# A hybrid decoder layer on one core: two loads on another queue, norms and gates behind minima, output products between turned tiles

## The chip, the cores and the metric

The kernel runs on one core of one Trainium2 chip. The metric is the device time of one execution in microseconds (us), the median over runs. The engines are named as in the profile: PE is TensorE, DVE is VectorE, ACT is ScalarE, POOL is GpSimd, SP is SyncE, which here only issues transfers.

## What is computed

One decoder layer for 1024 tokens of width 1024, all in float32:

```
xn  = rmsnorm(x);  proj = xn @ w_in          # one combined input projection
A:  8 heads, sliding window of 128, ALiBi, sinks, QK-norm, 2 kv heads
B:  8 heads, causal, logits + c[t] - c[s], c = cumsum(log_sigmoid(gate)), QK-norm
h   = x + concat[A, B] @ w_out
y   = h + relu(rmsnorm(h) @ w_up)^2 @ w_down
```

## The kernel before, in words

**Precision.** TensorE multiplies rounded operands. Each operand is therefore split: `hi` is the rounded value, `lo` the rest (`split`, line 75: a cast on one engine, line 77 or 79, and a subtraction on another, line 80). A product is three matmuls: hi x hi, hi x lo and lo x hi, each on a block of 128 x 128 weights.

**Stages, in order of time.**
- To about 38 us: x is loaded, scaled and split; the first part of the input projection (`w_a0`) fills eight PSUM banks `qps`, one for each block of 128 tokens. They are then copied to `q0` (line 227), on VectorE and ScalarE in turn.
- To about 79 us: `load_w` (line 237) brings the second weight `w_a1` in eight pieces. A piece is a load into a raw buffer `wr` (three buffers, issued by SP, line 241), a cast on ScalarE and a low part on GpSimd. `wa1_tile` (line 455) then makes the products of one block of tokens, 24 matmuls `ps`, copies the result to `q3`, and after every second block calls `qknorm` (line 266): a square on GpSimd (line 279), a sum on VectorE (line 284), a reciprocal root on ScalarE and VectorE, a multiplication on GpSimd (line 310). `make_q_a` and `make_k_a` turn (transpose on TensorE, then split) the normed heads. Meanwhile x is loaded again, row by row (`xq`, line 413), and squared for its norm.
- To about 318 us and on to 427 us: attention, in units. A unit is a score part (`scores_a`, `scores_b`: matmuls into one of two `sc` banks, then on VectorE the minimum of score plus bias, lines 544 and 699, then an exponential on ScalarE) and a mix part (`mix_a`, `mix_b`). `mix_b` takes the probabilities 256 keys at a time: up to four turns into one of three `tr` banks (line 740), `evict_pt` (a cast on ScalarE, line 402, and a low part on VectorE, line 403), then products with V into `pvb`. The mix parts run two units behind the scores (`pend`, `drain`, `DEPTH`). The last four units have 2, 4, 1 and 3 such steps (`ORDER_END`), on one head.
- `fillers` is a list of other work with a count of units from which each piece may be traced: the projections of the B heads (`project_b`) and the first half of the output products (`out_first`, over mixed tiles 0 to 3).
- To about 465 us: the second half of the output products (`out_products`, 24 matmuls `po` for one output tile, over mixed tiles 4 to 7), with `out_weights` (line 869) for their weights: a load into one of two raw buffers, a cast on ScalarE, a low part on GpSimd. `out_finish` (line 991) adds and splits h.
- From 465 us: the two products of the MLP, in a scheme with seven sub-products.

**Mixed tiles.** The mixed values of tiles 0 to 6 go through memory: `split_mix` (line 602) loads a tile, multiplies it by the reciprocals (`make`, line 624, on VectorE), splits it (ScalarE, GpSimd; there is one buffer `mixs` for the low half) and stores it; `load_mix` brings it back when TensorE wants it. `heads_b` runs one step of each tile's list for each unit. The last tile, 7, is split in place (line 763, ScalarE and VectorE).

**What sets the order.** Each engine runs its queue in order. The order is worked out by a scheduler that simulates expected times: of what is ready, it takes what has the highest priority, which is the order of the program, moved forward by `tc.high_priority(offset=...)`. `tc.issue_after(ins)` puts the instructions in its block behind `ins` on the engine of `ins`; it adds no wait of its own. So every edit of the program can move the order elsewhere too.

**Around the change.** Lines 227 to 229 copy `q0` and free the first banks; line 407 loads `w_a1`; line 463 calls `qknorm` after each second block; `start_a` (line 510) sets out the first stage; `forget_gates` (line 466) starts with an addition on VectorE, line 467; lines 934 to 957, at the end of attention, hold the start of the second output half:

```
    fill(True)
    mix6 = load_mix(6)
    ...
    beside(0, marks[-1], 4, 5)     # 12 products behind the last scores
    beside(1, ended[-1], 4)        # 6 behind the products of the last unit but two
    drain(1)
    beside(1, ended[-1], 5)
    drain(0)
```

## Time and profile before

| what | value |
|---|---|
| median of three runs | 1084.01 us (1082.84 to 1084.91) |
| the profiled execution | 1082.51 us |
| its span in the trace | 1080.8 us |
| matmuls on PE, and its busy time | 5492, 1070.7 us (99%) |
| busy time of DVE, ACT, POOL | 780.2, 573.4, 383.2 us |
| bytes moved | 195.93 MB, mean 181 GB/s |

A row of a view gives a start, a duration, the engine, the line of the kernel, the operation, what it writes and reads, and in brackets the idle time of the engine before it and what ended it. Rows of matmuls overlap, since they are pipelined; their count over the time that they fill gives their pace. In the table by stages each engine has its busy time and, in brackets, its number of instructions, in the order PE, PEld (weight loads), DVE, ACT, POOL; behind them stand the granted clock, the share of the DMA engines and their GB/s.

### The profile page before, as it was taken

The page shows a single profiled execution, that of the slowest core. Times are in us where ns is not written, and L with a number is a line of the kernel's source. Part 1 is how long each engine was busy: PE and PEld are TensorE (multiplying, and loading weights), DVE is VectorE, ACT ScalarE, POOL GpSimd, SP SyncE. Part 2 cuts the span into 40 slices and gives each one's busy share as a digit, 9 for nine tenths or more (in the row PEclk, how much of TensorE's full clock was granted, in tenths as well). Part 3 has the DMA queues.
Part 4 walks back from the last instruction along what each step waited for, and adds up shares of the span by engine and source line. Part 5 has one row for each costly group of instructions (what it writes and reads, how often), then busy time and mean ns, then how long its engine had stood idle before and what let it go on. Part 6 is the DMA issues. An engine that isn't in the chain of part 4 may idle for free.

```text
span 1080.8 us, 15581 instructions
## 1 busy us (share of the span) xinstructions
PE 1070.7 (99%) x5492; PEld 930.5 (86%) x5492; DVE 780.2 (72%) x1319; ACT 573.4 (53%) x1022; POOL 383.2 (35%) x350
## 2 busy tenths in 40 slices
PE   9999999999999999999999999999999999999998
PEld 8999999999998887888888888888888888888886
DVE  7377787877875787997777869674776876764495
ACT  5558587776767765655445453534533433333331
POOL 4572433546555663323233332322212313131100
PEclk9999999999999999999999999999999999999999
DMA  8401212324747656544454543443998885665423
GB/s 290 163 20 56 62 43 66 117 89 139 235 169 250 228 193 241 196 156 175 166 202 168 182 169 146 153 162 116 369 391 311 307 296 200 236 232 186 174 81 116
DMA packets 96366, 195.93 MB, mean 181 GB/s; under 512 B 7408, under 2 KB 19872, under 8 KB 96288
## 3 DMA queue, kind: packets, MB, share of 16 engines
q1 hardware_dynamic: 96000, 194.80, 51.2%
q8 instruction: 43, 0.70, 0.3%
q14 instruction: 35, 0.29, 0.1%
q10 hardware_dynamic: 288, 0.15, 0.0%
HBM read 141.87 MB, written 53.04 MB: 180 GB/s over the span
## 4 chain that ended last, share of the span: by engine, by line
PE 72%; DVE 2%; issue 1%; DMA 0%; ACT 0%; DVEq 0%; ACTq 0%
PE pu L73 28%; PE pd L73 28%; PE po L73 8%; PE pvb L73 2%; PE ps L73 2%; PE tpb L740 2%; PE spb L73 2%; DVE ptl L403 0%; DVE sb L699 0%; DMA mix_d<-mtb 0%; PE ptk L331 0%; DVE m L1040 0%; DVE pd L1333 0%; PE ptq L331 0%; PE pms L73 0%
## 5 line engine op out<-in xcount | busy, mean ns | idle before, releaser
L73 PE MATMUL pd<-hx,wx 128*128 128x512 f32 (+1 forms) x1350 | 304.9, 388 | 0.0
L73 PEld LDWEIGHTS pd<-hx,wx 128*128 128x128 f32 x1350 | 252.8, 188 | 52.1
L73 PE MATMUL pu<-bh,wu 128*128 128x512 f32 x896 | 276.6, 390 | 0.0
L73 PEld LDWEIGHTS pu<-bh,wu 128*128 128x128 f32 x896 | 168.2, 188 | 35.2 <-issue 0.2
L73 PE MATMUL ps<-w,x 128*128 128x384 f32 (+1 forms) x960 | 196.5, 342 | 0.6 <-ACT z L460 0.3
L73 PE MATMUL pu<-bl,wu 128*128 128x512 f32 x448 | 174.5, 389 | 0.0
L73 PEld LDWEIGHTS ps<-w,x 128*128 128x128 f32 x960 | 165.2, 188 | 4.8 <-POOL w L80 1.0
L77 ACT CAST hx<-hr 128x1024 fp32r<-128x1024 f32 x56 | 59.1, 1055 | 175.2 <-PE pd L73 171.0
L80 POOL TENSOR_TENSOR wx<-wda,wx 128x1024 fp32r<-128x1024 f32 x24 | 65.3, 2720 | 195.6 <-ACT wx L77 177.3
L80 DVE TENSOR_TENSOR hx<-hr,hx 128x1024 fp32r<-128x1024 f32 x56 | 72.3, 1299 | 71.0 <-ACT hx L77 71.0
L73 PEld LDWEIGHTS pu<-bl,wu 128*128 128x128 f32 x448 | 84.1, 188 | 18.0 <-DVE bl L978 0.3
L73 PE MATMUL po<-mix,wos 128*128 128x512 f32 x384 | 93.6, 393 | 0.0
L80 POOL TENSOR_TENSOR wu<-wus,wu 128x512 fp32r<-128x512 f32 x32 | 46.9, 1468 | 127.5 <-ACT wu L77 127.5
L73 PEld LDWEIGHTS po<-mix,wos 128*128 128x128 f32 x384 | 70.7, 188 | 13.8
L80 POOL TENSOR_TENSOR wu<-wur,wu 128x512 fp32r<-128x512 f32 x31 | 41.8, 1350 | 85.6 <-ACT wu L77 85.6
L77 ACT CAST wu<-wus 128x512 fp32r<-128x512 f32 x64 | 38.0, 618 | 58.9 <-PE pu L73 52.8
L1037 DVE TENSOR_TENSOR ht<-hb 128x512 f32<-128x512 f32 x32 | 22.9, 756 | 63.2 <-ACT hb L1145 63.2
L704 ACT ACTIVATE sb<-sb,nmb 128x128 f32<-128x128 f32 (+3 forms) x64 | 49.9, 779 | 26.3 <-DVE nmb L699 25.7
L403 DVE TENSOR_TENSOR ptl<-tpb,pth 128x512 fp32r<-128x512 f32 (+1 forms) x80 | 49.9, 630 | 17.5 <-ACT pth L402 16.6
L77 ACT CAST wx<-wda 128x1024 fp32r<-128x1024 f32 x56 | 58.5, 1049 | 7.6 <-DMA wda<-in_w_d_dram 7.6
L80 POOL TENSOR_TENSOR w<-wr,w 128x384 fp32r<-128x384 f32 (+1 forms) x47 | 49.9, 1070 | 28.6 <-ACT w L77 17.3
L694 POOL TENSOR_SCALAR_AFFINE_SELECT cm<-cb 128x128 f32<-128x128 f32 (+1 forms) x64 | 30.7, 479 | 57.5 <-DVE nmb L699 56.8
(207 smaller groups left out, 1837.7 us busy)
## 6 DMA issues: line engine op xcount, KB each, us to landing
wda<-in_w_d_dram SPq DMA_DIRECT2D x34, 1024.0 KB, 9.1
hr<-hid_d SPq DMA_DIRECT2D x56, 512.0 KB, 6.3
wur<-in_w_u_dram SPq DMA_DIRECT2D x32, 512.0 KB, 4.4
hid_d<-ht SPq DMA_DIRECT2D x16, 1024.0 KB, 4.3
hid_d<-hb SPq DMA_DIRECT2D x16, 768.0 KB, 3.6
mix<-mixs_d SPq DMA_DIRECT2D x7, 1024.0 KB, 5.8
wr<-in_w_b_dram SPq DMA_DIRECT2D x32, 192.0 KB, 2.4
xq<-in_x_dram SPq DMA_DIRECT2D x8, 512.0 KB, 5.7
```

What stands on the lines that cost most here:

```text
L73: return nc.tensor.matmul(out, lhsT, rhs, start=start, stop=stop)
L77: hi_eng.copy(hi, src)
L80: return lo_eng.tensor_tensor(out=lo, in0=src, in1=hi.bitcast(F32), op=ALU.subtract)
L403: nc.vector.tensor_tensor(out=lo[:, cols], in0=pt[:, cols], in1=hi[:, cols].bitcast(F32), op=ALU.subtract)
L694: nc.gpsimd.affine_select(out=cm, in_=bias, pattern=[[-1, n]], compare_op=ALU.is_ge, fill=BIG, base=n - P, channel_multiplier=1,)
L704: nc.scalar.activation(pr[:, :nk], pr[:, :nk], AF.Exp, scale=-1.0, bias=nm[:, c : c + 1], accum_out=dn_b[p % 2][:, h, i : i + 1] if p < 3 ...
L740: nc.tensor.transpose(tp[:, c0 : c0 + P], probs[qi][:, kb * P : (kb + 1) * P], ident)
L1037: eng.tensor_tensor(out=out, in0=a, in1=b, op=ALU.subtract)
```

## The change

Early:
- `load_w` and the loading of `w_a1` are traced ahead of the copies to `q0`. The loads of its last two pieces are issued by ScalarE, each behind the cast of the piece before it. ScalarE's copies of blocks 1, 3 and 5 stand behind the last cast, GpSimd's first square behind the last low part.
- The casts of the first B weight's later pieces stand behind the first unit's last exponential too.
- The norm of the last two blocks, and the turn that needs it, become a filler after two units; its sums, and the first addition of the gates, stand behind the second unit's last minimum.

Late:
- Both halves of mixed tile 6 are made in one step.
- The start of the second output half moves up, ahead of the mix part of the last unit but two. Of the second output pair, the six products of mixed tile 4 are put into that mix part: behind the turns of its second step and ahead of the turns of its third.
- The casts of the output weights from the eleventh on stand behind the last cast of mixed tile 7.

```diff
     def split(hi, lo, src, hi_eng, lo_eng):
...
+        cast = (hi_eng.copy if hi_eng is nc.scalar else hi_eng.tensor_copy)(hi, src)
+        split_casts[:] = [cast.ins]
         return lo_eng.tensor_tensor(out=lo, in0=src, in1=hi.bitcast(F32), op=ALU.subtract)
...
+    def load_w(src, n):
+        his, los = [], []
+        for k in range(KT):
+            wr, wh, wl = w_tiles(n)
+            late = not copied and k > 5
+            with tc.issue_after(split_casts[0]) if late else nullcontext():
+                (nc.scalar if late else nc.sync).dma_start(wr[:, :n], src[:, k, :])
+            with ExitStack() as behind:
+                for ins in (copied[-1], squared[-1], *exps[:1]) if copied and k > 2 else ():
+                    behind.enter_context(tc.issue_after(ins))
+                behind.enter_context(tc.high_priority(offset=HPO))
+                low = split(wh, wl, wr[:, :n], nc.scalar, nc.gpsimd)
+            split_of[:] = [split_casts[0], low.ins]
...
+    wa1 = load_w(w_a1, 392)
+    last_a1 = list(split_of)
+
     q0 = qk_t("q0")
     for t in LAST:
         eng = (nc.vector.tensor_copy, nc.scalar.copy)[t % 2]
-        eng(q0[:, t, :], qps[t][:, :384])
+        with tc.issue_after(last_a1[0]) if t in (1, 3, 5) else nullcontext():
+            eng(q0[:, t, :], qps[t][:, :384])
...
+            with tc.issue_after(last_a1[1]) if not squared else nullcontext():
+                square = nc.gpsimd.tensor_tensor(
...
+            with tc.issue_after(after) if after else nullcontext():
+                nc.vector.tensor_reduce(
...
-            if t % 2:
+            if t % 2 and t < NT - 1:
                 qknorm(q3, 6, t - 1, t + 1)
 
+    def last_norm():
+        with tc.high_priority(offset=HPA):
+            qknorm(q3, 6, NT - 2, NT, after=minima[1])
+        prep(make_q_a, 0, 1, 1)
+
     def forget_gates():
...
+        with tc.issue_after(minima[1]):
+            nc.vector.tensor_tensor(
...
-        prep(make_q_a, 0, 1, 1)
...
+        if e == KT - 2:
+            return [load, lambda: (make(0), make(1))]
         return [load, lambda: make(0), lambda: make(1)]
...
+            behind = hold.pop()(turned) if b > 1 and hold else None
+            with tc.issue_after(behind) if behind else nullcontext():
+                for qi in range(2):
...
+                        turned = nc.tensor.transpose(
...
-    def unit(score, mix):
+    def unit(score, mix, between=None):
         got = prep(score)
         pend.append(lambda: mix(got))
+        if between:
+            between()
         drain(DEPTH)
...
+    def outs_ahead():
+        for dt in (0, 4):
...
+            ahead_of.append((dt, ps, out_weights(dt, 4)))
+        fill(True)
+        beside(0, marks[-1], 4, 5)
+        hold.append(lambda turned: beside(1, turned, 4).ins)
...
+                outs_ahead if (p, u) == (3, 7) else None,
...
-        split(w[:, 0], w[:, 1], wr, nc.scalar, nc.gpsimd)
+        with tc.issue_after(mix_cast[0]) if i > 10 else nullcontext():
+            split(w[:, 0], w[:, 1], wr, nc.scalar, nc.gpsimd)
...
+    fillers.append((2, last_norm))
...
-    beside(0, marks[-1], 4, 5)
-    beside(1, ended[-1], 4)
     drain(1)
     beside(1, ended[-1], 5)
```

More of the change, by code (lines that the diff above doesn't have):

```diff
@@ L223, in hybrid_layer @@
             )
+    copied, squared, split_of, exps, minima = [], [], [], [], []
+    def load_w(src, n):
[11 more added lines that the diff above has]
+            split_of[:] = [split_casts[0], low.ins]
+            his.append(wh)
+            los.append(wl)
+        return his, los
+    wa1 = load_w(w_a1, 392)
+    last_a1 = list(split_of)
     q0 = qk_t("q0")
@@ L233, in hybrid_layer @@
     pd = psd.enter_context(tc.tile_pool(name="pd", bufs=2, space=PSUM, reuse_waits="tile"))
-    copied, squared = [], []
-    def load_w(src, n):
-        his, los = [], []
-        for k in range(KT):
-            wr, wh, wl = w_tiles(n)
-            nc.sync.dma_start(wr[:, :n], src[:, k, :])
-            with ExitStack() as behind:
-                for ins in (copied[-1], squared[-1]) if copied and k > 2 else ():
-                    behind.enter_context(tc.issue_after(ins))
-                behind.enter_context(tc.high_priority(offset=HPO))
-                split(wh, wl, wr[:, :n], nc.scalar, nc.gpsimd)
-            his.append(wh)
-            los.append(wl)
-        return his, los
     middle = []
@@ L264, in proj, with qknorm @@
         return ps
-    def qknorm(x, nh, tlo, thi, r=None):
+    def qknorm(x, nh, tlo, thi, r=None, after=None):
         n = thi - tlo
@@ L554, in scores_a @@
             )
+        exps.append(exp.ins)
+        minima.append(least.ins)
         marks.append(pe.ins)
@@ L733, in mix_b @@
             diag = b == qp
-            for qi in range(2):
-                for par in range(2):
-                    if diag and qi == 0 and par == 1:
-                        continue
-                    kb = 2 * b + par
-                    c0 = qi * 256 + (1 - par) * P
-                    nc.tensor.transpose(
-                        tp[:, c0 : c0 + P], probs[qi][:, kb * P : (kb + 1) * P], ident
-                    )
+            behind = hold.pop()(turned) if b > 1 and hold else None
+            with tc.issue_after(behind) if behind else nullcontext():
+                for qi in range(2):
+                    for par in range(2):
+                        if diag and qi == 0 and par == 1:
+                            continue
+                        kb = 2 * b + par
+                        c0 = qi * 256 + (1 - par) * P
+                        turned = nc.tensor.transpose(
+                            tp[:, c0 : c0 + P], probs[qi][:, kb * P : (kb + 1) * P], ident
+                        ).ins
             hi, lo = evict_pt(tp, slice(P if diag else 0, 512))
@@ L763, in mix_b @@
             last_mix.append(split(mh[7][r, ms], ml[7][r, ms], mt[r, :], nc.scalar, nc.vector))
+            mix_cast[:] = split_casts
     qkb = {}
     ended = []
-    mh, ml, mixt, last_mix = {}, {}, {}, []
+    mh, ml, mixt, last_mix, mix_cast, hold = {}, {}, {}, [], [], []
     pend = []
@@ L813, in heads_a, with beside @@
             fill()
+    ahead_of = []
+    def beside(n, mark, *es):
+        _, ps, w = ahead_of[n]
+        with tc.issue_after(mark):
+            return out_products(ps, w, es)
+    def outs_ahead():
+        for dt in (0, 4):
+            ps = first_banks() if dt == 0 else [
+                pa.tile([P, 512], F32, tag="sc", name=f"po{c}", bufs=2) for c in range(2)
+            ]
+            ahead_of.append((dt, ps, out_weights(dt, 4)))
+        fill(True)
+        beside(0, marks[-1], 4, 5)
+        hold.append(lambda turned: beside(1, turned, 4).ins)
     splitting = []
@@ L819, in heads_b @@
             qp, h = (ORDER_END if p == 3 and u > 3 else ORDER_B)[u % 4], u // 4
-            unit(lambda: scores_b(p, qp, h), lambda got, qp=qp, h=h: mix_b(got, p, qp, h))
+            unit(
+                lambda: scores_b(p, qp, h), lambda got, qp=qp, h=h: mix_b(got, p, qp, h),
+                outs_ahead if (p, u) == (3, 7) else None,
+            )
             if u == 1:
@@ L897, in out_products @@
                 cs = slice(c * 512, (c + 1) * 512)
-                mm(ps[c], wl[:, j, :], mh[e][:, cs], False, j == 3)
+                pe = mm(ps[c], wl[:, j, :], mh[e][:, cs], False, j == 3)
+        return pe
     def first_banks():
@@ L935, in hybrid_layer @@
     mix6 = load_mix(6)
-    ahead_of = []
-    for dt in (0, 4):
-        ps = first_banks() if dt == 0 else [
-            pa.tile([P, 512], F32, tag="sc", name=f"po{c}", bufs=2) for c in range(2)
-        ]
-        ahead_of.append((dt, ps, out_weights(dt, 4)))
-    def beside(n, mark, *es):
-        _, ps, w = ahead_of[n]
-        with tc.issue_after(mark):
-            out_products(ps, w, es)
-    beside(0, marks[-1], 4, 5)
-    beside(1, ended[-1], 4)
     drain(1)
```

27 lines of the change are left out of this document (10 added, 17 removed).

## The prediction

> **What bounds the kernel now.** I read the page first, then the table of busy time by stages, then the order of time of each engine in the two stages that the edits touch, backwards from each idle stretch of TensorE.
>
> ```profile
> span 1080.8 us, 15581 instructions
> PE 1070.7 (99%) x5492; PEld 930.5 (86%) x5492; DVE 780.2 (72%) x1319; ACT 573.4 (53%) x1022; POOL 383.2 (35%) x350
> ...
> 38.00:60.00 22.00, 21.47 (x124) 20.67 (x124) 13.37 (x32) 11.09 (x31) 15.69 (x18) 1.00 0.12 37
> 60.00:82.00 22.00, 21.25 (x130) 20.23 (x127) 16.67 (x45) 11.63 (x34) 15.43 (x17) 1.00 0.09 28
> 82.00:262.00 180.00, 179.81 (x1165) 172.45 (x1164) 135.30 (x361) 133.86 (x340) 75.54 (x91) 1.00 0.25 77
> 409.00:427.00 18.00, 16.23 (x105) 13.66 (x104) 14.30 (x32) 11.70 (x27) 6.45 (x6) 1.00 0.55 198
> 427.00:465.00 38.00, 38.00 (x169) 31.43 (x168) 34.16 (x53) 20.66 (x34) 9.48 (x7) 1.00 0.64 231
> ```
>
> TensorE sets the time. The change takes no product and no turn (a PE transpose) away from it, so all it can win is TensorE's idle time. In the stage table the first pair is the stretch and PE's busy time: from 38 to 82 us PE lacks 0.53 + 0.75 = 1.28 us, from 409 to 427 us it lacks 1.77 us, and the stages beside them lack 0.19 and 0.00. The granted clock is 1.00 in all of them. So the prize is 3.05 us of printed idle. It is a little more in truth, because rows of products overlap: 24 products fill 5.69 us where each row alone lasts about 0.39 (rows below), so one follows another every 0.23 us, and a stall costs its printed idle and some 0.15 more. With four stalls early and two and some small ones late, the most that the edits can win is about 1.8 us early and 2.3 us late, 4.1 us in all. A bound of the time from below is thus 1084.0 - 4.1 = 1079.9, give or take the spread of the medians.
>
> **The late edit.** TensorE at the end of attention, then VectorE, ScalarE and GpSimd in the same stretch:
>
> ```profile
> 410.79 1.54 PE L73 MATMUL po<-mix,wos 128*128 128x512 f32 x6
> 412.17 1.03 PE L740 MATMUL tpb<-ident,sb 128*128 128x128 f32 x8
> 412.96 1.62 PE L73 MATMUL po<-mix,wos 128*128 128x512 f32 x6
> ...
> 415.19 0.28 PE L73 MATMUL pvb<-ptl,vb 128*128 128x128 f32 x1
> 416.11 0.52 PE L740 MATMUL tpb<-ident,sb 128*128 128x128 f32 x3 [0.64 <-DVE dnb L711]
> 417.63 1.16 PE L740 MATMUL tpb<-ident,sb 128*128 128x128 f32 x7 [1.00 <-DVE ptl L403]
> ...
> 421.20 1.65 PE L73 MATMUL po<-mix,wos 128*128 128x512 f32 x6
> 422.68 0.49 PE L740 MATMUL tpb<-ident,sb 128*128 128x128 f32 x3
> ...
> 425.14 0.39 PE L73 MATMUL pvb<-pth,vb 128*128 128x256 f32 x1
> ...
> 426.61 5.69 PE L73 MATMUL po<-mix,wos 128*128 128x512 f32 x24
> 403.30 0.67 DVE L624 TENSOR_TENSOR mixr<-mixr,mixn 128x512 f32<-128x512 f32 x1
> 413.92 1.44 DVE L624 TENSOR_TENSOR mixr<-mixr,mixn 128x512 f32<-128x512 f32 x1
> 415.28 0.68 DVE L403 TENSOR_TENSOR ptl<-tpb,pth 128x512 fp32r<-128x512 f32 x1
> 416.81 1.27 DVE L403 TENSOR_TENSOR ptl<-tpb,pth 128x512 fp32r<-128x512 f32 x2
> 411.66 0.62 ACT L77 CAST wos<-wor 128x512 fp32r<-128x512 f32 x1
> 427.72 0.40 ACT L77 CAST mix<-mtb 64x256 fp32r<-64x256 f32 x1 [0.48 <-DVE mtb L755]
> 404.70 2.08 POOL L80 TENSOR_TENSOR mixs<-mixr,mixn 128x512 fp32r<-128x512 f32 x1 [1.53 <-ACT mixn L77]
> 406.74 0.39 POOL L694 TENSOR_SCALAR_AFFINE_SELECT cm<-cb 128x256 f32<-128x256 f32 x1
> 413.27 1.53 POOL L80 TENSOR_TENSOR wos<-wor,wos 128x512 fp32r<-128x512 f32 x1
> ```
>
> Both stalls, 0.64 and 1.00 us, end when VectorE has taken a low part (ptl, line 403) out of a turned tile: there are three such banks, and the next turns need one back. (The first is printed against a reciprocal, but the low part of 415.28 ends at 415.96, 0.15 us before the turns start.) VectorE is late because line 624 stands ahead of that low part and takes 1.44 us, where the same operation took 0.67 us at 403.30. GpSimd's operation of 413.27 to 414.80, the low part of a *later* weight, lies beside it.
>
> The skill has a rule for this. In the Trainium skill, page "SBUF — State Buffer", the port section says that VectorE and GpSimd share a port pair as an exclusive lock, so the loser stands still for the other's whole instruction. The trace agrees: 414.80 + 0.67 is 415.47, and line 624 ends at 415.36. By that rule the moved half could pay the 1.44 us again at its new place, beside the 2.08 us of GpSimd at 404.70.
>
> Step by step, the change does four things here.
>
> 1. Both halves of the sixth mixed tile are made in one step, a unit of scores earlier. Line 624's 1.44 us leave the place ahead of the low part. At the new place, behind 403.30, they cost VectorE between 0.67 and 1.44 us; TensorE has first output products there, so I price that at nothing, and at most at 1.4 us if that cover is missing. ScalarE's cast and GpSimd's low part of that half move along.
>
> 2. The later output weight's cast (411.66) and its low part (413.27) go behind the last mixed cast (427.72). They cost nothing as long as they are done before their product. That product starts 24 products after 426.61, at 426.61 + 24 x 0.23 = 432.1; the cast can start at 428.1, and with 0.62 + 1.53 the low part ends by 430.3. That is 1.8 us of cover. The load after next needs that weight's raw buffer and so moves to about 430 as well; its product is 5.4 us later still.
>
> 3. Six products of the second output pair (now at 421.20, 1.48 us until the next row) go between the turns of the longest unit's second and third tile (now the eight turns of 412.17, in one go). TensorE is full from 410.79 to about 415.3. With six products more (1.38 us, as from 410.79 to 412.17) and the three turns of 416.11 (0.34) it would reach the seven turns of 417.63 at 415.3 + 1.38 + 0.34 = 417.0. They can start if the two low parts now at 416.81 come 0.6 us sooner, and edits 1 and 2 take 1.44 us out of VectorE's queue ahead of them. That is 417.63 - 417.0 = 0.6 us won at this point, with 1.4 us of products already behind it: 2.0 us.
>
> 4. What is late next: from 417.6 to 426.6 the six products no longer stand between turns of 420.8 and 422.68. The last unit's own chain (turn, cast, low part) then has 1.4 us less cover. If it needs all of it back, the gain falls to 0.6; if the small wait before 425.14 goes too, it rises to 2.3. VectorE has idle time (it is busy for 14.30 of the stage's 18.00 us), and six more products of the same pair remain, so I take **1.9 us**, range 0.6 to 2.3.
>
> **The early edit.** TensorE's four stalls, and the rows behind the first and the last:
>
> ```profile
> 38.36 4.07 PE L73 MATMUL ps<-w,x 128*128 128x392 f32 x22
> 42.70 7.57 PE L73 MATMUL ps<-w,x 128*128 128x392 f32 x41 [0.27 <-POOL w L80]
> 58.15 0.39 PE L73 MATMUL sp<-k1a,q1a 128*128 128x256 f32 x1 [0.26 <-DVE q1a L324]
> 67.99 3.12 PE L73 MATMUL ps<-w,x 128*128 128x392 f32 x16 [0.29 <-ACT z L460]
> 78.20 0.36 PE L73 MATMUL sp<-k1a,q1a 128*128 128x256 f32 x1 [0.46 <-DVE nm_a L544]
> 40.60 1.06 POOL L279 TENSOR_TENSOR sq<-q 128x512 f32<-128x512 f32 x1
> 41.63 1.01 POOL L80 TENSOR_TENSOR w<-wr,w 128x392 fp32r<-128x392 f32 x1
> 35.16 2.14 SPq L241 DMA_DIRECT2D wr<-in_w_a_dram  x2
> 37.13 0.50 ACT L77 CAST w<-wr 128x392 fp32r<-128x392 f32 x1
> 40.79 0.53 ACT L77 CAST w<-wr 128x392 fp32r<-128x392 f32 x1
> wr<-in_w_b_dram SPq DMA_DIRECT2D x32, 192.0 KB, 2.4
> 78.52 0.90 DVE L467 TENSOR_TENSOR z<-z,vt 128x64 f32<-128x64 f32 x1
> ```
>
> The stall at 42.4 waits for the last weight's low part, which stands behind a square on GpSimd (40.60, 1.06 us) and behind a cast that ScalarE makes only at 40.79, after copies of q0. The change puts copies and square behind them; that alone would win the 0.27 us and its overlap, 0.4. Against it stands the move of the two loads: they now leave at 35.16 and within 2.14 us of it. On ScalarE the first can leave only with the cast before it, at 37.1. A load of this size lands after 2.4 us (the row of the next weights): 39.5, cast 39.6, second load 39.6, landed 42.0, cast to 42.5, low part 1.01 to 43.6. That is 0.9 us *later* than the 42.64 of now. If TensorE keeps its order, this stall grows from 0.27 to about 1.2; if the order puts the next tile's products ahead (they are independent, on another bank, and the order is worked out from expected times), it goes to nothing. So -0.9 to +0.4; I take +0.1. The first norm's square then starts about 3 us later, with the weight's eight tiles of 24 products as its cover; I price that at nothing, and at 1.3 us if the turns behind the 41 products of 42.70 come late.
>
> A rule of the Trainium skill speaks against this part: page "DMA: Bandwidth & Descriptors", section "Issuing engines are not separate DMA queues", says that transfers begun by different engines share the same 16 DMA engines and that spreading them saves only issue time. By it the ScalarE loads win no landing time at all, and the early sum would hold the ordering alone, 0.4 in place of 0.1 for this stall if the loads then land as early as now.
>
> At the other end the last pair's norm and the gates' first addition go behind the minima of the second unit. VectorE's 0.90 us at 78.52 stand between the first and second unit's minima now; the stall of 0.46 before 78.20 waits for the first unit's. I expect half to all of that stall and of a smaller wait after it to go: +0.5, range 0 to 0.7. The stalls at 58 and 68 are not touched by any edit, but the whole order of the engines is worked out anew. Early sum: **+0.6**, range -1.5 to +1.4.
>
> **The sum** against the profiled execution, 1082.5 (its span of 1080.8 and 1.7 around it): 1082.5 - 1.9 - 0.6 = 1080.0. Its time was 1.5 us under the median of the three runs, 1084.0, so for the median I say 1084.0 - 2.5 = 1081.5. The measurement can tell about 0.2%, or 2.2 us, from no change, so the forecast stands just beyond it.
>
> **The rivals.** *All six waits go*, early and late: 1079.5 to 1080. For it: each has one releaser that an edit names or that shifts with it. Against: two of the early ones are not named. *The gain is given back*, either late (the last unit's chain wants its 1.4 us of cover again: gain 0.6 + 0.6, 1082.8) or early (the late load holds TensorE 0.9 us longer and the norms another 0.6: 1.9 - 1.5 = 0.4, 1083.6). For it: the landing time above. This is also the case that the early edit does not do what it says, for its loads land later. *Slower, by GpSimd's queue*: there is one buffer for the low half of a mixed tile, so the second half's low part has to wait until the first's store has landed.
>
> ```profile
> mixs_d<-mixs SPq DMA_DIRECT2D x2, 256.0 KB, 2.8
> 406.81 0.32 SPq L627 DMA_DIRECT2D mixs_d<-mixs  x1
> ```
>
> That store leaves at 406.81 and lands about 2.8 us later, at 409.6. If the second low part (2 us) stands ahead of the mask now at 406.74, the mask, the last unit's minima and everything behind them move from 406.74 to 411.6, 4.9 us; less the 1.4 us that VectorE wins, the end of attention moves 3.4 us back: with +0.6 early, 1084.0 + 3.4 - 0.6 = 1086.8. It decides from the point where that low part is queued ahead of the mask; the order would have to misjudge the landing by 2 us, so I hold it unlikely.
>
> **How the numbers follow.** The forecast (late 1.9, early about 0.6): 0.43. All waits gone: 0.13. Given back, one way or the other: 0.33. Slower by GpSimd's queue or a like disorder: 0.11. Faster by over 0.2%, below 1081.8, takes most of the first case and all of the second, and a few upsets aside gives 0.55; the same, 0.34; slower, 0.11. The range goes from 1079.2 (all waits gone and a favourable median) to 1084.6 (early loss with a small late gain).
>
> **What would show it.** Late: line 624 has no row after 410 us; a run of six products stands between turned tiles before 415; the idle times of 0.64 and 1.00 are gone from 409 to 427 us; the casts of later weights stand behind the last mixed cast. Early: two DMA issues on ScalarE near 37 and 39.6 us, the last low part near 43.6, no wait on it on TensorE. The forecast is wrong if the stage up to 427 us still lacks over a microsecond of TensorE, if the last low part holds TensorE for a microsecond, or if stages between 82 and 409 us, which no edit names, lose or win more than 0.7 us by the new order.

## The result and the profile after

The changed kernel takes 1085.76 us (median of 20 runs, 1084.02 to 1089.65), the kernel before 1082.9 us beside it (20 runs, 1081.8 to 1086.37): a ratio of 1.0028, 95% interval 1.002 to 1.0035. It is about 3 us slower, and outside the range of 1079.2 to 1084.6. (The forecast started from a median of three runs, 1084.0; with 20 runs the kernel before lies 1.1 us lower.) A second series gave 1.0017 [1.0008, 1.0027]. The profiled execution took 1085.18 us, with a span of 1083.4 us. The page of the changed kernel begins:

```profile
span 1083.4 us, 15572 instructions
...
PE 1072.0 (99%) x5492; PEld 930.8 (86%) x5492; DVE 781.8 (72%) x1319; ACT 574.9 (53%) x1022; POOL 382.4 (35%) x350
```

TensorE has the same 5492 products and turns, so what is new is waiting. The table by stages of the changed kernel, in the same stretches as before:

```profile
38.00:60.00 22.00, 21.25 (x123) 20.36 (x122) 12.04 (x27) 8.35 (x24) 15.97 (x18) 1.00 0.15 44
60.00:82.00 22.00, 21.36 (x130) 20.46 (x129) 17.25 (x48) 14.69 (x40) 14.03 (x17) 1.00 0.09 27
...
409.00:427.00 18.00, 15.58 (x96) 12.48 (x95) 13.69 (x31) 11.66 (x27) 5.04 (x5) 1.00 0.73 268
427.00:465.00 38.00, 38.00 (x175) 31.65 (x174) 34.74 (x49) 20.09 (x33) 11.09 (x8) 1.00 0.54 183
```

From 38 to 60 us TensorE lacks 0.75 us where it lacked 0.53; to 82 us 0.64 instead of 0.75. From 409 to 427 us it lacks 2.42 us, where 1.77 were to shrink. A stage's row can't show a gain or loss that is carried on from the stage before it. So I also measured a *lag*: each matmul gets the pace of its width in the kernel before (0.2265 us for 512 columns, 0.177 for 392, about 0.174 for 384, 0.1185 for 256, 0.109 for 128), and the two kernels are compared at the time when the same sum of these paces (equal work) is behind them. The full sum is the same in all kernels here, about 1060 us. A wait "of pace" is the time between two starts less this pace, so it is somewhat longer than the printed idle time. What each stage adds to the lag, worked out so from one trace of each kernel ("start" is the lag at 20 us of work, and "early" goes from there to 100):

| us, + is later than before | start | early, to 100 us of work | 100 to 390 | end of attention, 390 to 420 | join, 420 to 500 | sum |
|---|---|---|---|---|---|---|
| changed kernel | +0.29 | 0.00 | -0.17 | +1.35 | +1.19 | +2.66 |
| changed kernel, second series | +0.45 | -0.15 | -1.20 | +0.77 | +1.22 | +1.09 |
| early edits only | +0.62 | -0.07 | -0.57 | +1.35 (clock) | +0.27 | +1.60 |
| early edits, loads on SyncE | +0.52 | -1.39 | +0.37 | +0.06 | +0.30 | -0.14 |
| late edits only | +0.54 | +1.35 | -0.73 | +0.70 | +1.19 | +3.05 |
| changed, loads on SyncE | +0.36 | -1.73 | +0.14 | +2.09 | +1.19 | +2.07 |
| changed, later weights free | +0.77 | +0.36 | -0.63 | +0.97 | -0.05 | +1.42 |
| changed, six products put back | +0.38 | +0.10 | -0.64 | -0.56 | +1.17 | +0.44 |
| changed, 12 products behind value products | +0.46 | +0.34 | +0.60 | +1.02 | +1.17 | +3.59 |
| changed, halves apart | +0.11 | +3.19 | +0.39 | +0.85 | +1.51 | +6.05 |
| changed, second low buffer | +0.38 | +1.54 | -0.85 | 0.00 | +1.21 | +2.28 |
| before + weights behind the last mixed cast | +0.41 | -0.08 | 0.00 | -0.79 | +1.33 | +0.87 |
| before + both halves in one step | +0.08 | -0.22 | -0.51 | +1.73 (clock) | -0.23 | +0.86 |
| changed, three parts undone | +0.72 | -1.03 | +1.12 | -0.11 | -0.07 | +0.64 |
| the same, one weight behind | +0.96 | -1.71 | -1.18 | +0.47 | -0.05 | -1.50 |
| early on SyncE + one weight | +0.85 | -0.36 | -0.40 | -0.29 | +0.53 | +0.33 |

No edit names the column 100 to 390, and two executions of the same changed kernel have -0.17 and -1.20 there; I read it as spread. The starts and some early numbers move with the landings of loads, too, and a profiled execution can lie far from its kernel's median (ninth experiment: 1088.56 us, median 1085.3). So one row's sum isn't the kernel's time (the ratios below are), but a stage whose number comes back with the same waits says where a cost lies. In the changed kernel it is the end of attention and the join, 2.0 to 2.5 us, beside an early stage that wins nothing.

**Early.** The orders around the last two weights of the changed kernel, by engine:

```profile
36.77 0.34 ACTq L232 DMA_DIRECT2D wr<-in_w_a_dram  x1
...
39.15 0.52 ACT L78 CAST w<-wr 128x392 fp32r<-128x392 f32 x1 [0.39 <-DMA wr<-in_w_a_dram]
39.18 0.33 ACTq L232 DMA_DIRECT2D wr<-in_w_a_dram  x1
...
42.01 0.52 ACT L78 CAST w<-wr 128x392 fp32r<-128x392 f32 x1 [1.60 <-DMA wr<-in_w_a_dram]
...
42.66 1.02 POOL L80 TENSOR_TENSOR w<-wr,w 128x392 fp32r<-128x392 f32 x1 [1.82 <-ACT w L78]
...
42.58 0.19 PEld L73 LDWEIGHTS ps<-w,x 128*128 128x128 f32 x1 [0.36 <-ACT w L78]
43.73 1.52 PE L73 MATMUL ps<-w,x 128*128 128x392 f32 x7 [0.71 <-POOL w L80]
```

Load, cast, load, cast now stand one behind the other: 36.77 to 39.15, then 39.18 to 42.01, and the low part ends at 43.68. Before, both loads had left SyncE by 37.3. TensorE waits for the cast and then for the low part, about 1.2 us with the overlap.

Of the other three early stalls, the two that the prediction held for untouched, at 58.15 and 67.99 us, are gone; a wait of 0.31 us of pace is new at 64.23. The one that was to shrink, before the second unit's scores, has grown from 0.46 to 0.58 us:

```profile
78.63 0.36 PE L73 MATMUL sp<-k1a,q1a 128*128 128x256 f32 x1 [0.58 <-DVE nm_a L557]
```

**End of attention.** TensorE, VectorE, ScalarE and GpSimd of the changed kernel:

```profile
410.26 0.39 PE L73 MATMUL pvb<-ptl,vb 128*128 128x256 f32 x1 [0.20 <-DVE ptl L412]
...
413.55 3.01 PE L73 MATMUL po<-mix,wos 128*128 128x512 f32 x12
...
416.76 0.36 PE L73 MATMUL pvb<-pth,vb 128*128 128x256 f32 x1
...
418.91 1.17 PE L759 MATMUL tpb<-ident,sb 128*128 128x128 f32 x7 [0.66 <-DVE ptl L412]
...
422.49 0.52 PE L759 MATMUL tpb<-ident,sb 128*128 128x128 f32 x3
424.39 0.38 PE L73 MATMUL pvb<-pth,vb 128*128 128x256 f32 x1 [1.38 <-DVE mtb L774]
...
404.04 1.27 DVE L639 TENSOR_TENSOR mixr<-mixr,mixn 128x512 f32<-128x512 f32 x2
...
405.91 1.11 DVE L80 TENSOR_TENSOR mix<-mtb,mix 64x256 fp32r<-64x256 f32 x1
...
414.47 0.47 DVE L716 CUSTOM_DVE_ANT_0 sb<-spb,cm,nmb 128x256 f32<-128x256 f32 x1
...
418.07 1.29 DVE L412 TENSOR_TENSOR ptl<-tpb,pth 128x512 fp32r<-128x512 f32 x2 [0.89 <-ACT pth L411]
...
423.92 0.42 DVE L774 TENSOR_TENSOR mtb<-pvb,mtb 64x256 f32<-64x256 f32 x1
...
417.45 1.07 ACT L411 CAST pth<-tpb 128x512 fp32r<-128x512 f32 x2 [1.15 <-PE pvb L73]
...
423.19 0.37 ACT L773 COPY mtb<-pvb 64x256 f32<-64x256 f32 x1
...
405.44 1.30 POOL L80 TENSOR_TENSOR mixs<-mixr,mixn 128x512 fp32r<-128x512 f32 x1 [1.52 <-ACT mixn L78]
...
411.29 1.31 POOL L80 TENSOR_TENSOR mixs<-mixr,mixn 128x512 fp32r<-128x512 f32 x1 [1.13 <-DMA mixs_d<-mixs]
412.54 0.41 POOL L711 TENSOR_SCALAR_AFFINE_SELECT cm<-cb 128x256 f32<-128x256 f32 x1
```

Read the stall at 418.91 backwards: VectorE's low part (418.07) had waited for ScalarE's cast (417.45), and this one for the value products (pvb) that begin at 416.76 and give back a high buffer, `pth`, of which there are three. These value products stand behind the run of 12 products that begins at 413.55. Six of them are the moved ones. The low part is still late, no longer because of VectorE's queue but because of what the six products pushed back. And six fewer products stand between 421 and 424 us, where now the value products of the last unit but one wait 1.38 us for the bank that ScalarE (423.19) and then VectorE (423.92) empty. The time from the last start of the unit before to these value products is hardly new: 422.38 to 424.39 us, before 420.70 to 422.93. Before, the six products filled it, and no wait over 0.3 us stood there.

The same lag cut finer, by us of work: ahead of the turns, at the turns where both stalls of before were, and at the value products behind them.

| us, + is later than before | 390 to 404 | turns, 404 to 408 | value products, 408 to 420 |
|---|---|---|---|
| changed kernel | +0.96 | -1.46 | +1.84 |
| changed kernel, second series | +0.39 | -1.46 | +1.85 |
| late edits only | +0.33 | -1.46 | +1.83 |
| changed, six products put back | +0.30 | -1.10 | +0.24 |
| before + weights behind the last mixed cast | -0.01 | -0.76 | -0.02 |

The late edits do win at the turns, and lose more behind them. The first column is a third loss, between about 408 and 411 us (row of 410.26). Kernels with the halves apart have it as well (+0.32, +0.48 and +0.49 in the first, ninth and twelfth experiment), the sixth and seventh do not (+0.08 and -0.01). Which edit brings it is not separated.

**Join.** TensorE, VectorE and GpSimd of the changed kernel, then the corresponding rows of the kernel before:

```profile
466.25 0.39 PE L73 MATMUL pu<-bh,wu 128*128 128x512 f32 x1
...
468.94 0.50 PE L73 MATMUL pu<-bl,wu 128*128 128x512 f32 x1 [0.27 <-DVE bl L1009]
...
475.39 0.50 PE L73 MATMUL pu<-bl,wu 128*128 128x512 f32 x1 [0.48 <-DVE bl L1009]
...
430.08 0.69 DVE L1071 TENSOR_TENSOR wus<-wur 128x512 f32<-128x512 f32 x1
430.69 1.78 DVE L1068 TENSOR_TENSOR wus<-wur 128x512 f32<-128x512 f32 x1
432.39 1.77 DVE L1068 TENSOR_TENSOR wus<-wus,wur 128x512 f32<-128x512 f32 x1
...
430.32 3.30 POOL L80 TENSOR_TENSOR wos<-wor,wos 128x512 fp32r<-128x512 f32 x2 [14.61 <-ACT wos L78]
```

```profile
464.78 0.39 PE L73 MATMUL pu<-bh,wu 128*128 128x512 f32 x1
...
429.96 0.72 DVE L1040 TENSOR_TENSOR wus<-wur 128x512 f32<-128x512 f32 x1 [1.38 <-DMA wur<-in_w_u_dram]
430.60 0.68 DVE L1037 TENSOR_TENSOR wus<-wur 128x512 f32<-128x512 f32 x1
...
428.85 1.28 POOL L80 TENSOR_TENSOR wos<-wor,wos 128x512 fp32r<-128x512 f32 x1 [10.84 <-ACT wos L77]
```

The first up product is 1.47 us later than before, as much as the end of attention. Then two waits for `bl` come, 0.43 and 0.65 us of pace. The low parts of the later weights now run from 430.32 to 433.62, beside VectorE's sums for the up weights (line 1068). Each of these takes 1.77 to 1.78 us where it took 0.68. VectorE is nearly full from there to 470 us (34.74 of 38.00 us), so it carries 2.2 us towards the join. It had begun 1.35 us sooner after TensorE's last value product (2.11 us behind it, before 3.46), which leaves about 0.9; the join loses 1.19.

### The profile page after: what moved, and what is told of

The parts are those of the page before. It is cut to its first block, busy times and chain, and to the rows that moved or that the text cites. A ratio compares the mean times of both kernels' runs of the same rounds, so it can differ in the third digit from the quotient of the medians.

```text
span 1083.4 us, 15572 instructions
## 1 busy us (share of the span) xinstructions
PE 1072.0 (99%) x5492; PEld 930.8 (86%) x5492; DVE 781.8 (72%) x1319; ACT 574.9 (53%) x1022; POOL 382.4 (35%) x350
## 4 chain that ended last, share of the span: by engine, by line
PE 87%; DVE 6%; DMA 3%; issue 1%; POOL 1%; ACT 1%; SPq 0%; ACTq 0%; DVEq 0%; POOLq 0%
PE pd L73 28%; PE pu L73 27%; PE ps L73 14%; PE po L73 4%; PE spb L73 3%; PE pvb L73 3%; PE tpb L759 3%; PE sp L73 1%; PE tpa L580 1%; PE pv L73 1%; DMA xq<-in_x_dram 1%; DMA wr<-in_w_a_dram 1%; DVE x L207 1%; PE ptk L340 1%; DVE h L1029 1%
## 5 line engine op out<-in xcount | busy, mean ns | idle before, releaser
L80 DVE TENSOR_TENSOR hx<-hr,hx 128x1024 fp32r<-128x1024 f32 x56 | 74.6, 1340 | 71.4 <-ACT hx L78 71.4
```

Source lines behind the costliest of these rows:

```text
L80: return lo_eng.tensor_tensor(out=lo, in0=src, in1=hi.bitcast(F32), op=ALU.subtract)
```

## The experiments

**1. Early edits alone.** The kernel before with the early edits and none of the late ones.

> The kernel before with the early edits alone. Theory (the loss is late: at the end of attention about 1.3 us and at the start of the up products about 1.2 us): within 0.5 us of before; TensorE waits about 1.2 us near 42.6 us for the last low part, and no up product waits for a low part of h near 470 us. Rival (the early edits or a reordering in general cost the time): 1 to 3 us slower than before.

Measured: 1083.63 us, 1.0004 [0.9994, 1.0015]. The early edits as a whole do nothing to the time that can be told. In the trace TensorE loses about 1.2 us at 42.8 us to the two loads and is level again by 100 us of work.

**2. Late edits alone.** The kernel before with the three late edits and none of the early ones.

> The kernel before with the late edits alone. Theory: 2.3 to 3.0 us slower than before, with the waits at the end of attention and near 470 us as in the changed kernel. Rival (early edits to blame): at most 1 us slower.

Measured: 1084.86 us, 1.001 [1.0001, 1.0019]. The same waits as in the changed kernel stand at the end of attention (0.91 and 1.63 us of pace), and the same 1.19 us at the join. So these waits are the late edits' own. The time is 1.1 us over before by the ratio (1.6 by the medians), less than the 2.3 to 3.0 expected.

**3. The later weights' casts free again.**

```diff
-        with tc.issue_after(mix_cast[0]) if i > 10 else nullcontext():
-            split(w[:, 0], w[:, 1], wr, nc.scalar, nc.gpsimd)
+        split(w[:, 0], w[:, 1], wr, nc.scalar, nc.gpsimd)
```

> The changed kernel with the later output weights' casts left free, as before. Theory (their low parts now lie on GpSimd beside VectorE's sums of the up weights, 1.78 us each where they took 0.68, and that lateness holds up the up products): the waits near 469 and 475 us go, about 1.2 us faster than the changed kernel, so 1.5 to 1.9 us slower than before. Rival (those waits come from the later end of attention): they stay, 2.6 to 3.1 us slower than before.

Measured: 1084.62 us, 1.0008 [0.9995, 1.002], 0.9 us over before by the ratio, where the theory had 1.5 to 1.9. VectorE in this kernel:

```profile
430.69 1.78 DVE L1067 TENSOR_TENSOR wus<-wur 128x512 f32<-128x512 f32 x1
432.39 0.68 DVE L1067 TENSOR_TENSOR wus<-wus,wur 128x512 f32<-128x512 f32 x1
```

One of the two collisions is left, and the join's waits are gone (-0.05 us in place of +1.19). One such delay fits into VectorE's earlier start, the second doesn't.

**4. The two loads back on SyncE's queue**, nothing else.

```diff
-            late = not copied and k > 5
+            late = False
```

> The changed kernel with the last two pieces loaded by SP again; everything else in the same order. Theory: the loads leave about 2 us earlier, TensorE's wait near 42.6 us falls from about 1.2 to at most 0.3 us; of the 0.9 us some comes back as waits for scores near 64 and 78 us, so 0.3 to 0.9 us faster than the changed kernel. Rival (the loads' queue makes no difference, since transfers share the same engines): the wait stays at about 1.2 us.

Measured: 1083.01 us, 0.9998 [0.9989, 1.0007]. SyncE, GpSimd and TensorE in this kernel:

```profile
35.02 2.15 SPq L232 DMA_DIRECT2D wr<-in_w_a_dram  x2
...
39.40 2.15 POOL L80 TENSOR_TENSOR w<-wr,w 128x392 fp32r<-128x392 f32 x2 [0.76 <-ACT w L78]
...
38.72 12.25 PE L73 MATMUL ps<-w,x 128*128 128x392 f32 x68
```

Both loads have left by 37.2, the last low part ends at 41.55 instead of 43.68, and TensorE runs 68 products without a gap. The early stage wins 1.73 us: 0.55 at this stall, 0.44 and 0.57 at those of 58 and 68 us, nothing at that of 78. In the time, 2 to 3 us of the changed kernel's loss go, more than the 0.3 to 0.9 expected. The five traces with the loads on SyncE (4, 6, 12, 13, 14) win 0.36 to 1.73 us early, those with the loads on ScalarE 0.15 at most. So the loads on ScalarE cost what the rest of the early order wins. Which part of that order took the stalls of 58 and 68 us is not separated.

**5. The changed kernel once more**, as the measure beside the next three.

> The changed kernel once more, beside the others on one chip. If its loss is a property of its order: 1.002 to 1.0035 of before, a wait of 1 to 1.3 us near 42.6 us and two waits of together 1.2 us near 469 and 475 us again. If chips or landings of transfers make it: within 0.1% of before, and the waits of the early stage differ.

Measured: 1084.88 us, 1.0017 [1.0008, 1.0027], with the same waits: 0.97 us of pace at 42.6, 0.91 and 1.63 at 416 to 423, 0.43 and 0.61 at the join.

**6. Early edits alone, loads on SyncE**, by the edit of the fourth.

> The kernel before with the early edits alone, but all loads on SP. Theory (the ordering behind casts and minima wins about 1.6 us by 82 us, the ScalarE loads take it away): TensorE 1.3 to 2 us ahead of before from 82 to 320 us, and 0.5 to 1.6 us faster in the end. Rival (attention's end is set by VectorE's chain, so an early gain is waited away there): ahead by as much up to 320 us, and within 0.4 us of before in the end.

Measured: 1081.85 us, 0.9991 [0.9982, 1.0], against 1.0004 with the loads on ScalarE. The early stage wins 1.39 us, and about 1 us is left in the time; the interval touches 1.

**7. Only the weights' casts, on the kernel before.**

```diff
-        split(w[:, 0], w[:, 1], wr, nc.scalar, nc.gpsimd)
+        with tc.issue_after(mix_cast[0]) if i > 10 else nullcontext():
+            split(w[:, 0], w[:, 1], wr, nc.scalar, nc.gpsimd)
```

> The kernel before, only with the later output weights' casts behind the last mixed cast. Theory (port shared by GpSimd and VectorE): VectorE's sums of the up weights take about 1.8 us each beside GpSimd's two low parts, TensorE waits about 1.2 us in all for low parts of h near 468 and 474 us; 1.0 to 1.4 us slower than before, less up to 0.5 us if the end of attention wins by the low part that has left it. Rival (they only come with the later end of attention): no such waits, same as before.

Measured: 1083.11 us, 0.9999 [0.999, 1.0007]. VectorE at the end of attention and at the start of its sums:

```profile
414.25 0.67 DVE L624 TENSOR_TENSOR mixr<-mixr,mixn 128x512 f32<-128x512 f32 x1
...
429.61 0.69 DVE L1042 TENSOR_TENSOR wus<-wur 128x512 f32<-128x512 f32 x1 [1.49 <-DMA wur<-in_w_u_dram]
430.22 1.78 DVE L1039 TENSOR_TENSOR wus<-wur 128x512 f32<-128x512 f32 x1
```

At the end of attention this edit alone wins 0.79 us: line 624 takes 0.67 us instead of 1.44, and the stall before the three turns is gone. At the join it loses 1.33. VectorE's sums wait for the up weight's load, so they begin hardly sooner (429.61, before 429.96), and one collision of 1.1 us goes through to TensorE. So the theory's waits came, and the win at the end of attention hides them in the time.

**8. Only both halves in one step, on the kernel before.**

```diff
+        if e == KT - 2:
+            return [load, lambda: (make(0), make(1))]
```

> The kernel before, only with both halves of the sixth mixed tile in one step. Theory (the second half's multiplication lies beside GpSimd's low part and GpSimd waits for the one low buffer's store ahead of a mask): the last scores 0.3 to 1 us later, the end of attention 0 to 0.8 us later. Rival (VectorE wins 1.4 us ahead of the low parts, as predicted): the stalls of 0.64 and 1.00 us near 416 us shrink by over half, 0.5 to 1.4 us faster.

Measured: 1083.38 us, 1.0004 [0.9994, 1.0014]. A row of VectorE, TensorE's stall, and the table by stages around it:

```profile
415.33 1.48 DVE L80 TENSOR_TENSOR mix<-mtb,mix 64x256 fp32r<-64x256 f32 x1
...
417.56 1.62 PE L742 MATMUL tpb<-ident,sb 128*128 128x128 f32 x7 [1.85 <-DVE ptl L403]
```

```profile
417.00:418.00 1.00, 0.44 (x3) 0.31 (x3) 1.00 (x2) 0.00 (x0) 0.00 (x0) 1.00 0.99 406
418.00:419.00 1.00, 1.00 (x6) 0.94 (x6) 0.50 (x3) 0.40 (x1) 0.00 (x0) 0.52 1.05 410
...
420.00:421.00 1.00, 1.00 (x7) 1.00 (x6) 0.56 (x1) 0.63 (x2) 0.00 (x0) 0.50 0.80 250
```

The two stalls of before (0.89 and 1.24 us of pace) have merged into one of 2.10. Line 624 is gone from its place, but another operation of VectorE now lies beside GpSimd's low part of the later weight (414.95 to 416.53) and takes 1.48 us where it took 0.40, so the low parts come at 416.74 instead of 416.81. In this execution the granted clock then falls to 0.50; most of the stage's +1.73 us is that.

**9. The changed kernel with the halves apart.** The two lines of the eighth removed.

> The changed kernel with the sixth mixed tile's halves in two steps again, as before. Theory (the half's edit puts VectorE and GpSimd in each other's way ahead of the last scores, the placed products cost the rest): the last scores 0.3 to 0.6 us earlier than in the changed kernel, TensorE's waits near 417 and 422 us still there, 0.2 to 0.6 us faster than it. Rival (the halves' edit is the whole loss at the end of attention): those waits gone, over 1 us faster than it.

Measured: 1085.3 us, 1.0026 [1.0015, 1.0036]. The waits of 0.91 and 1.63 us are still there, and it is not faster than the changed kernel. The halves' step isn't what makes the changed kernel slow.

**10. The six products put back** behind the products of the last unit but two.

```diff
-        hold.append(lambda turned: beside(1, turned, 4).ins)
...
+    beside(1, ended[-1], 4)
```

> The changed kernel with the six products of the second output pair back behind the last unit but two, not between its turns. Theory (taken away there they no longer cover the last units' chain): the wait near 423 us, 1.6 us, falls to at most 0.4 us, and that near 417 us, 0.9 us, grows to at most 1.9; the end of attention 0.2 to 1.2 us earlier than in the changed kernel. Rival (the chain of ScalarE and VectorE sets the end whatever TensorE does): the sum of the waits, and the end, stay within 0.2 us.

Measured: 1084.2 us, 1.0017 [1.0006, 1.0027]. TensorE in this kernel:

```profile
416.70 1.17 PE L759 MATMUL tpb<-ident,sb 128*128 128x128 f32 x7 [0.74 <-DVE ptl L412]
...
420.29 1.60 PE L73 MATMUL po<-mix,wos 128*128 128x512 f32 x6
...
422.19 0.38 PE L73 MATMUL pvb<-pth,vb 128*128 128x256 f32 x1
```

The six products stand at 420.29 again, and the wait of 1.63 us near 423 is down to 0.21 (row of 422.19). The end of attention gains 0.56 us instead of losing 0.77 to 1.35. In the finer table, from 404 us of work on, it gains 0.86 us instead of losing 0.4: the move itself costs about 1.25 us in the trace. The runs' times do not show this cost, since the ratio is not below that of the fifth experiment, which has the same early and join losses.

**11. Twelve products behind the value products** that give back the buffers, instead of ahead of them.

```diff
-        beside(0, marks[-1], 4, 5)
-        hold.append(lambda turned: beside(1, turned, 4).ins)
+        beside(0, marks[-1], 4)
+        pv_end = ended[-1]
+        beside(0, pv_end, 5)
+
+        def held(turned):
+            with tc.issue_after(pv_end):
+                return beside(1, turned, 4).ins
+
+        hold.append(held)
```

> The changed kernel with twelve products (the first pair's second six and the placed six) behind the value products of the unit before, not ahead of them. Theory (those value products hold the buffers of evicted tiles; behind twelve products they release them 2.3 us later, ScalarE then takes out the next tile late): the tile after them is taken out 0.8 to 1.5 us earlier than in the changed kernel, the wait near 418 us falls below 0.4 us, the end of attention 0.4 to 1 us earlier. Rival (VectorE alone is late): the wait stays at about 0.9 us.

Measured: 1085.78 us, 1.0023 [1.0013, 1.0033]. The wait at 418 is gone, and one of 1.19 us of pace stands ahead of those value products instead; the one of 1.62 stays. TensorE:

```profile
415.81 0.38 PE L73 MATMUL pvb<-pth,vb 128*128 128x256 f32 x1 [1.01 <-DVE mtb L774]
```

There are 18 products to lay over three waits; in these traces each place that gets six fewer shows its wait.

**12. A version made of what won.** Early edits with the loads on SyncE, on the kernel before, and the cast of one later weight behind the third from last mixed cast.

```diff
+            mix_cast.extend(split_casts)
...
-        split(w[:, 0], w[:, 1], wr, nc.scalar, nc.gpsimd)
+        with tc.issue_after(mix_cast[-3]) if i == 11 else nullcontext():
+            split(w[:, 0], w[:, 1], wr, nc.scalar, nc.gpsimd)
```

> The early edits with loads on SP, and of the late ones only that the first later output weight's cast waits, for the last mixed cast but two. Theory: early 1.3 us, the end of attention 0.5 to 0.8 us as in the run with the weights behind the last mixed cast, and no wait of up products near 470 us, since that low part falls into GpSimd's idle time before 428 us: 1.2 to 2.2 us faster than before. Rival (what is won early is waited away later): within 0.7 us of before.

Measured: 1081.3 us, 0.9985 [0.9976, 0.9993]. It beats both kernels, by as much as expected, though not with the expected parts: its trace wins 0.36 us early and 0.29 at the end of attention, and loses 0.53 at the join, where no wait was expected.

**13. Three parts undone in the changed kernel**: the edits of the third, fourth and tenth together.

> The changed kernel with three of its parts undone at once: the two loads go back to SyncE's queue, the six products go back behind the last unit but two, and the later weights' casts are free again. What stays of the change is the early order of copies, squares, norm and gates, both halves of mixed tile 6 in one step, and the output products' start a step earlier. Theory (three separate costs that add up: the loads' 1.4 to 1.7 us, the products' about 1.5, the casts' 1.2 less the 0.8 that they win at the end of attention): 1085.8 less about 3.5, that is 0.9983 to 0.9996 of the kernel before, TensorE ahead of it by 0.8 to 1.7 us until 400 us, no wait over 0.5 us between 422 and 425 us and none over 0.4 us at the start of the join. Rival (the costs overlap, and what is left, the halves in one step above all, costs as much by itself): 1.0005 or more, with the wait near 416 us still there and the end of attention over 0.5 us later in equal work than its start.

Measured: 1081.4 us, 0.9986 [0.9975, 0.9997]. With the three parts undone the loss is gone: from +3.0 us (second series +1.8) to -1.5, as the sum of three costs had it. The join loses nothing, the value products of the last unit but one wait 0.21 us instead of 1.63, the early stage wins 1.03. TensorE is not ahead until 400 us, though: the trace lost 1.12 us between 100 and 390. What stays is a stall of 1.48 us of pace near 418, where the kernel before has two, 2.1 us in all. The sixth experiment, without any late edit, is at 0.9991 [0.9982, 1.0], so what remains of the late edits is not shown to win anything.

**14. The same with one weight behind**, by the edit of the twelfth.

> As the run before it, but one later output weight's cast (the eleventh) stays behind a mixed cast, the third from last, the other weights are free. Theory (the casts help at the end of attention by taking one low part of GpSimd's away from beside VectorE's mixed tile, and harm only where the last of them reach the join): 0.3 to 0.8 us below the run before it, 0.9980 to 0.9992 of the kernel before. Rival (with both halves in one step the mixed tile's sum no longer lies beside that low part, so that the cast has nothing left to win): within 0.3 us of the run before it, or above it.

Measured: 1081.53 us, 0.9988 [0.9977, 1.0], no better than the run before it, and the end of attention +0.47. The rival was right: with both halves in one step, the weight's cast has nothing left to free.

**15. A second buffer for the low half** of the second half of mixed tile 6.

```diff
-            lo = ap2.tile([P, 512], F32R, tag="mixs", name="mixs", bufs=1)
+            lo = ap2.tile([P, 512], F32R, tag="sq" if (e, c) == (KT - 2, 1) else "mixs", name="mixs", bufs=1)
```

> The changed kernel, but the low part of mixed tile 6's second half goes to another buffer, so that on GpSimd it no longer waits for the store of the first half; the mask of the last unit then comes earlier than at 412.54 us. Theory (the wait for the store is the late start of the last unit's minima, but TensorE waits in this stretch for banks and for the unit's own chain): last minimum 1 to 2 us earlier than 414.47 us, end of attention 0 to 0.8 us earlier, 1.0015 to 1.0028 of the kernel before. Rival (GpSimd's wait for the store is what makes the end of attention late, as the slower case of the prediction has it): end of attention 1.0 us or more earlier, 1.0012 or less.

Measured: 1084.72 us, 1.0013 [1.0001, 1.0024]. Neither theory's premise came true. GpSimd made both low parts one behind the other, but then took the sums of an output part ahead of the mask, which came at 414.53, later than in the changed kernel; the last minimum came at 415.59. And yet the end of attention lost nothing, 0.8 to 1.35 us better than the changed kernel, which is the rival's size without its mechanism. TensorE's order came out different as well, with three of the products between the value products and the turns, and no wait there; the wait at the value products behind them stays, 1.38 us. So a late mask need not cost anything. What the wait for the store costs alone, with TensorE's order kept, stays open.

## Why the prediction was wrong

**The late sum of 1.9 us has two terms, and neither held.** The kernel was to be 2.5 us faster and is 2.9 us slower by the medians. The third step has 2.0 us won at the turns, and the fourth takes 0.1 us back for the place that the six products leave. In equal work the changed kernel won 1.46 us at the turns and lost 1.85 at the place left, the same in three traces.

**The fourth step is off the most.** It named the cover and priced its loss at 1.4 us as the bad case, and took 0.1. "VectorE has idle time" and "six more products of the same pair remain" were no reasons for that: the value products of the last unit but one wait for a bank, which a copy on ScalarE and an operation on VectorE have to empty first, one behind the other. That takes about as long as before; only the cover is gone. It cost 1.38 us printed, 1.63 of pace, and with the six products put back 0.21 is left.

**The third step, "that is 417.63 - 417.0 = 0.6 us won at this point, with 1.4 us of products already behind it: 2.0 us"**, wanted the two low parts 0.6 us sooner than 416.81. They came at 418.07, 1.26 us later. It followed VectorE's queue up to the low parts but not what TensorE's own queue holds behind the six products: the value products gave back the `pth` buffers about 2.3 us later (416.76, before 414.42), ScalarE's cast waited for them, and the low parts for the cast. Of the 1.46 us won at the turns, 1.10 are there without the six products as well; moving them won 0.36 and lost 1.6.

**The second step, that the later weights' casts "cost nothing as long as they are done before their product", failed by its criterion.** The product was never late. The low parts got VectorE's sums as neighbours: 2 x 1.1 us, and the join lost 1.19 (nothing without the edit). Its use at the end of attention was real: 0.79 us on the kernel before. The rule of the shared port (the Trainium skill, "SBUF — State Buffer", section "Who interferes with whom") was weighed for the first step only; the trace agrees with it here, 1.78 us beside GpSimd against 0.68 alone, and it should have been asked of every low part that the change moves.

**The first step was about right in its cost and wrong in its use.** At the new place VectorE pays 0.6 for the second half and 0.71 for a neighbour's low part (405.91, 1.11 instead of 0.40). That TensorE pays nothing there is not shown: it lost 0.3 to 1.0 us between 408 and 411 us, but kernels without this edit lost some there too. And alone the step freed no low part: it merged two stalls.

**The early edit.** The chain of the two loads was priced right, 43.6 us against 43.68, and the wait as about 1.2. The value taken from "-0.9 to +0.4" was +0.1, on the hope that the order would put other products ahead; TensorE kept its order, and this stall alone cost 0.74 us in equal work. At the other end the forecast of +0.5 met about +0.7 from 44 to 86 us of work, but by luck: the stall before 78.20 that it named is still there, 0.58 us at 78.63, and the gain lies at the stalls of 58 and 68 us, "not touched by any edit". The early sum, forecast as +0.6, was 0.0. The rule that spreading loads over issuing engines saves only issue time (the Trainium skill, "DMA: Bandwidth & Descriptors", section "Issuing engines are not separate DMA queues") spoke against this part. The trace agrees in that nothing landed sooner, and goes beyond it: each load was tied to a cast on its engine, and that cost 1.3 to 1.7 us against the traces with the loads on SyncE (experiments 6 and 4).

**The rivals.** "The gain is given back" is what happened, on both sides at once, and beyond zero. The slower rival's mechanism appeared: GpSimd's low part waited 1.13 us for the store, and the mask came at 412.54, 2.1 us later than before (410.40; the last minimum 414.47, before 412.18):

```profile
410.40 0.40 POOL L694 TENSOR_SCALAR_AFFINE_SELECT cm<-cb 128x256 f32<-128x256 f32 x1 [1.27 <-DVE nmb L699]
```

But this is not shown to cost anything: with the mask later still, the fifteenth run lost nothing there. The kernel is slower, as that rival had it, but not for its reason. Stages between 82 and 409 us, finally, moved by more than the 0.7 us allowed, in both directions and in kernels of the same order: that test was too sharp for one trace each.

## What to carry to other kernels

Moving cover to a stall opens the place that it came from, and on an in-order engine it also delays what stands behind its new place; follow each resource that the delayed work gives back (here three buffers). Ask of each moved operation not only whether its user can wait, but which operation of another engine becomes its neighbour, and whether that one is on a full engine. A load issued from a compute engine's queue inherits that queue's order: two loads behind two casts are one chain.

## What the runs showed of the hardware

**Behind a short stall the granted clock was halved, in some executions.** In the eighth experiment the granted clock is 1.00 through the stall and 0.50 to 0.52 for the 3 us behind it (rows above); 256-column products then start every 0.21 us instead of 0.12. In the first the same follows the same double stall (0.50 from 419 to 421 us), and in the ninth the early waits (0.50 from 46 to 48 us). Before the drop TensorE had been idle for 1.85 us in one go (eighth), or for about half of 4 us (ninth). Of the kernel before, 40 of 128 executions have a mean granted clock of 0.998 or less and take 1084.1 us on average, the others 1082.7. Of the changed kernel, 7 of the first 20 do, 1088.0 against 1085.3. In the kernels with neither the late double stall of before nor the early wait for the two loads (experiments 2, 4, 7, 12, 13, 14) none of 69 do; in the other experiments 26 of 100. The late waits of 0.91 and 1.63 us alone (experiments 2 and 4) brought none in 22. So some waits of a microsecond or two seem to cost more than themselves, in up to a third of the executions. The Trainium skill ("TensorE: Matmul & The Clock Gate", section "Why this matters for your kernels") warns of idle gaps over about 3 us; here the clock fell behind gaps below 2 us, in some executions. That the stalls are the cause is argued from where the drops lie and which kernels lack them.

**Landing times moved the early stage.** The first of the two loads took 2.4 us from issue to cast in the changed kernel and 3.9 us in the ninth run (37.49 to 41.42), and the early stage then lost 3.2 us, part of it by the clock.
